# Holding activations instead of weights: a decoder layer on one core, with results kept with tokens on the partitions

## The chip, the core and the metric

The kernel runs on one core of a Trainium2 chip. Its five engines run their own instruction streams and wait for each other through semaphores: TensorE (matrix products, the profile's PE, with its loads of the stationary operand as PEld), VectorE (DVE), ScalarE (ACT), GpSimd (POOL) and SyncE (SP), which here issues nearly all loads. A matrix product holds one operand (stationary, up to 128 x 128) and moves the other past it (up to 512 columns), and writes to PSUM. The metric is device time in microseconds (us) of one execution.

## What is computed

One decoder layer for 256 tokens of 2048 features in f32. Cut to what matters:

```python
h = rmsnorm(x, ffn1_norm);  x = x + 0.5 * swiglu(h, ffn1_w_gate, ffn1_w_up, ffn1_w_down)   # 2048 -> 5632 -> 2048
h = rmsnorm(x, mix_norm);   proj = h @ w_in                                                # 2048 -> 9728
q_a, k_a, v_a, q_b, f_b, i_b, og_b, gate_a, gate_b = split(proj)
out_a = sliding_window_attention(rope(q_a), rope(k_a), v_a, sinks)                         # 256 x 1024
out_b = rmsnorm(hgrn2(q_b, f_b, i_b, lb)) * silu(og_b)                                     # 256 x 1024
merged = sigmoid(gate_a) * (out_a @ w_up_a) + sigmoid(gate_b) * (out_b @ w_up_b)
x = x + merged @ w_out
h = rmsnorm(x, ffn2_norm);  x = x + 0.5 * swiglu(h, ffn2_w_gate, ffn2_w_up, ffn2_w_down)
x = x + sigmoid(rmsnorm(x, ple_norm) @ ple_w_gate) * (p @ ple_w_proj)
return rmsnorm(x, final_norm)
```

## The kernel before

All weights stream through once, in a fixed order (`weight_order`), as 780 pieces of 128 x 1024 numbers (512 KB). `Weights.prep` loads a piece (SP), ScalarE rounds it to 12 bits (`whi`), VectorE takes the difference (`wlo`); `AHEAD = 4` pieces are prepared before the one in use, in rings of 6, 5 and 5 buffers. Activations are split the same way into two parts. A product is the sum of three: high by high, low by high, high by low.

There are two forms. In `chunk_b` and `pair_b` (through `mm_b`, L304, L306, L308) a 128 x 128 block of weights is stationary, and both parts of 256 tokens move past it as 512 columns, then past the low part of the weights as 256 columns. The result has features on the partitions and tokens along the row, which is the layout that the next product needs. `evac_b` adds the two halves and multiplies by the row factor of the norm, which `broadcast_cols` has laid out along the row (`rB`). In `block_a` (through `mm_a`, L270, L271, L276) a 128 x 128 block of activations is stationary and 512 weight columns move; the result has tokens on the partitions.

Gate, up and down of both feed-forwards, w_f, w_q, the two gates, w_up_a, w_up_b and w_out use the first form; w_i, w_og, w_kv, w_qa and the last stage the second. The residual x lies as `xT`, features on the partitions, until `natural` turns it with transposes (L778) before the last stage. `token_sums` adds squares over partitions with small matmuls (L231). The feed-forward runs in two slices of the 5632 columns: gate and up of a slice, then down of that slice, added to x. `next_stage` scales each finished part of x and splits it for the next product. While weights stream, `pump` advances attention and the recurrence, one step of each queue between two pieces, and `W.later(n, fn)` runs a step before the n-th piece from there.

Of the kernel before, what the change touches and what calls it, by code (L numbers as in the profile page):

```python
# [25 lines left out]
AHEAD = 4  # L26
PRIO = 3000
# [68 lines left out]
FF_SLICES = [(0, 24), (24, 44)]  # L96
MIX = (
    ("fq", 0), ("fq", 1), ("i", 0), ("og", 0), ("kv", 0), ("fq", 2),
    ("q", 0), ("fq", 3), ("q", 1), ("i", 1), ("og", 1),
)  # L100
GLOOK = 2


def weight_order():
# [9 lines left out]
    def ffn(n):  # L114
        if n == 1:
            for kg in range(4):
                for hf in range(2):
                    add("start", kg, hf)
        for a, b in FF_SLICES:
            for c in range(a, b):  # L120
                if n == 1 and c < 2:
                    continue
# [15 lines left out]
    for f in range(-GLOOK, KC):  # L138
        if f + GLOOK < KC:
            for w in ("w_ga", "w_gb"):  # L140
                for hh in range(2):
                    add(w, f + GLOOK, hh)
        if f >= 0:
            add("w_ua", f, 0)
            add("w_ub", f, 0)
    for fp in range(8):
        block("w_out", fp, 4)
# [8 lines left out]
def decoder_layer(ctx: ExitStack, tc: tile.TileContext, io, out):  # L156
# [17 lines left out]
    def atile(shape=(P, 2, S), dt=F32R, name="act"):  # L174
        return sb.tile(list(shape), dt, tag="act", name=uid(name), bufs=32)

    def etile(shape=(P, 2, S), name="e"):
        return sb.tile(list(shape), F32, tag="e", name=uid(name), bufs=4)
# [17 lines left out]
    xT = [sb.tile([P, 2, S], F32, tag=f"xT{i}", name=f"xT{i}") for i in range(8)]  # L196
    xc = lambda f: xT[f // 2][:, f % 2]
# [7 lines left out]
    def split_scaled(dst, src, g, vector=False):  # L205
        """dst[:, 0] + dst[:, 1] = src * g, each part of 12 bits."""
# [10 lines left out]
    def add_squares(ssq, src, first):  # L217
        """ssq += src ** 2, by feature."""
        if first:
            nc.scalar.activation(ssq, src, AF.Square)  # L220
        else:
            sq = gtile([P, 2, S], name="sq")
            nc.scalar.activation(sq, src, AF.Square)
            nc.vector.tensor_tensor(ssq, ssq, sq, op=ALU.add)

    def token_sums(ssq):
        """[128, 2, 1]: the sums over the features of each token, in PSUM."""
        ps = misc([P, 2, 2], uid("sq"))
        nc.vector.tensor_tensor(ssq[:, 0], ssq[:, 0], ssq[:, 1], op=ALU.add)
        for t in range(2):  # L230
            nc.tensor.matmul(ps[:, t], ssq[:, 0, t * P:(t + 1) * P], ones[:, 0:2], start=True, stop=True)  # L231
        return ps[:, :, 0:1]

    def inv_rms(ss, stage):
        """[128, 2]: 1 / sqrt(mean + eps) of each token."""
        r = const.tile([P, ss.shape[1]], F32, name=f"rstd{stage}")
        if ss.shape[2] > 1:
            nc.vector.tensor_reduce(r, ss, axis=AX.X, op=ALU.add)
        else:
            nc.vector.tensor_copy(r.unsqueeze(2), ss)  # L240
# [79 lines left out]
    def ffn(n, hT, rB_of, on_pair):  # L320
# [12 lines left out]
        for si, (a, b) in enumerate(FF_SLICES):  # L333
# [17 lines left out]
            for fp in range(8):  # L351
# [3 lines left out]
                if si == len(FF_SLICES) - 1:  # L355
                    on_pair(fp)
# [555 lines left out]
```

## Time and profile before

| | |
|---|---|
| time, median of 3 runs | 2264.26 us (2264.09 to 2264.36) |
| span of the profiled execution, first to last instruction | 2262.8 us |
| TensorE busy | 2245.5 us (99%), 12996 matmuls |
| loads of the stationary operand | 1943.7 us (86%), beside matmuls |
| VectorE, ScalarE, GpSimd busy | 1447.5 us (64%), 1090.3 us (48%), 11.8 us (1%) |
| moved from and to memory | 417.21 MB, 184 GB/s on average |
| granted TensorE clock | 0.999 of full speed |

The span begins with the first and ends with the last instruction that the profile shows; what lies around it is in the time and not in the span. Matmuls are pipelined: one starts before the one ahead has ended, so the distance between starts tells the cost, not the duration of one.

### The profile page before, as it was taken

What the parts mean: (1) busy time and instruction counts of PE and PEld (TensorE: products, weight loads), DVE (VectorE), ACT (ScalarE), POOL (GpSimd) and SP (SyncE); (2) the same over time, 40 slices, a digit from 0 to 9 for tenths busy, and PEclk for the clock granted to TensorE, in tenths of its full rate; (3) what the DMA queues carried; (4) which work ended last, traced back from release to release, by engine and by line L of the source; (5) the groups of instructions that cost most, each with busy time, mean ns of one, the idle gap of its engine ahead of it and who ended that gap; (6) DMA issues with size and microseconds to landing.
All of it is one profiled execution on the core that took longest, in us unless ns stands there. A gap on an engine that the chain in (4) does not pass through costs nothing.

```text
span 2262.8 us, 33350 instructions
## 1 busy us (share of the span) xinstructions
PE 2245.5 (99%) x12996; PEld 1943.7 (86%) x12996; DVE 1447.5 (64%) x2172; ACT 1090.3 (48%) x1590; POOL 11.8 (1%) x25
## 2 busy tenths in 40 slices
PE   8999999999999999999999999999999999999998
PEld 7888888888888878878888888888888888888887
DVE  7667655666666765776666677666665566666665
ACT  6455433444444445556445544544443344444444
POOL 0000000000000000000000000000000000000000
PEclk9999999999999999999999999999999999999999
DMA  7556565555665555444555555555555555556653
GB/s 276 191 189 192 186 190 188 187 188 187 188 190 190 177 159 168 159 133 157 186 186 187 187 189 188 187 188 187 188 189 191 186 186 186 188 189 215 186 179 110
DMA packets 116942, 417.21 MB, mean 184 GB/s; under 512 B 13616, under 2 KB 14000, under 8 KB 116784
## 3 DMA queue, kind: packets, MB, share of 16 engines
q1 hardware_dynamic: 115920, 413.74, 56.4%
q8 instruction: 102, 1.67, 0.3%
q10 hardware_dynamic: 864, 1.35, 0.2%
q14 instruction: 56, 0.46, 0.1%
HBM read 412.94 MB, written 2.10 MB: 183 GB/s over the span
## 4 chain that ended last, share of the span: by engine, by line
PE 99%; ACT 0%; issue 0%; DMA 0%; DVE 0%; SPq 0%; ACTq 0%; POOLq 0%; POOL 0%
PE pb L304 36%; PE pb L306 20%; PE pp L304 16%; PE pp L306 9%; PE pa L270 4%; PE pa L271 4%; PE pa L276 4%; PE pb L308 3%; PE pp L308 1%; PE lv L642 1%; PE st L304 1%; PE st L306 0%; PE sc L562 0%; DMA xT<-in_xT 0%; PE po L601 0%
## 5 line engine op out<-in xcount | busy, mean ns | idle before, releaser
L83 DVE TENSOR_TENSOR wlo<-raw,whi 128x1024 fp32r<-128x1024 f32 (+1 forms) x781 | 954.5, 1223 | 747.7 <-ACT whi L82 744.9
L82 ACT CAST whi<-raw 128x1024 fp32r<-128x1024 f32 (+1 forms) x781 | 818.4, 1049 | 1035.2 <-issue 252.6
L304 PE MATMUL pb<-hTf,whi 128*128 128x512 f32 x2580 | 710.6, 394 | 0.0
L304 PEld LDWEIGHTS pb<-hTf,whi 128*128 128x128 f32 x2580 | 449.6, 189 | 61.8
L306 PEld LDWEIGHTS pb<-hTf,wlo 128*128 128x128 f32 x2752 | 421.0, 188 | 59.0
L306 PE MATMUL pb<-hTf,wlo 128*128 128x256 f32 x2752 | 436.8, 280 | 0.0
L304 PE MATMUL pp<-act,whi 128*128 128x512 f32 x1344 | 369.2, 394 | 0.0
L304 PEld LDWEIGHTS pp<-act,whi 128*128 128x128 f32 x1344 | 233.0, 189 | 32.0
L306 PEld LDWEIGHTS pp<-act,wlo 128*128 128x128 f32 x1408 | 215.8, 189 | 30.2
L306 PE MATMUL pp<-act,wlo 128*128 128x256 f32 x1408 | 223.8, 281 | 0.0
L304 PE MATMUL pb<-hTmx,whi 128*128 128x512 f32 x720 | 200.2, 396 | 0.0
L304 PEld LDWEIGHTS pb<-hTmx,whi 128*128 128x128 f32 x720 | 124.8, 189 | 18.0 <-issue 0.7
L306 PEld LDWEIGHTS pb<-hTmx,wlo 128*128 128x128 f32 x768 | 117.4, 188 | 16.6
L306 PE MATMUL pb<-hTmx,wlo 128*128 128x256 f32 x768 | 121.8, 280 | 0.0
L270 PE MATMUL pa<-whi,hTmx 128*128 128x512 f32 x224 | 91.7, 409 | 0.0
L271 PE MATMUL pa<-whi,hTmx 128*128 128x512 f32 x224 | 87.7, 392 | 0.0
L314 DVE TENSOR_TENSOR ff<-ff,rBf 128x256 f32<-128x256 f32 x174 | 73.9, 425 | 5.7
L289 DVE SCALAR_TENSOR_TENSOR xT<-pp,xT 128x256 f32<-128x256 f32 x160 | 67.4, 422 | 7.7 <-PE pp L308 2.4
L312 DVE TENSOR_TENSOR ff<-pb,ff 128x256 f32<-128x256 f32 x172 | 71.9, 418 | 0.0
L308 PE MATMUL pb<-hTf,whi 128*128 128x512 f32 x172 | 68.1, 396 | 0.0
L304 PE MATMUL pp<-mT,whi 128*128 128x512 f32 x240 | 66.1, 394 | 0.0
L311 ACT COPY ff<-pb 128x256 f32<-128x256 f32 x172 | 63.1, 367 | 0.0
(234 smaller groups left out, 1683.2 us busy)
## 6 DMA issues: line engine op xcount, KB each, us to landing
raw<-in_ffn_down SPq DMA_DIRECT2D x176, 512.0 KB, 3.4
raw<-in_ffn_gate SPq DMA_DIRECT2D x172, 512.0 KB, 3.4
raw<-in_ffn_up SPq DMA_DIRECT2D x172, 512.0 KB, 3.3
raw<-in_w_ga SPq DMA_DIRECT2D x32, 512.0 KB, 3.4
raw<-in_w_gb SPq DMA_DIRECT2D x32, 512.0 KB, 3.3
raw<-in_w_out SPq DMA_DIRECT2D x32, 512.0 KB, 3.3
raw<-in_ple_gate SPq DMA_DIRECT2D x32, 512.0 KB, 4.3
raw<-in_w_f SPq DMA_DIRECT2D x16, 512.0 KB, 3.5
```

What stands on the lines that cost most here:

```text
L82: nc.scalar.copy(hi[:, c], raw[:, c])
L83: nc.vector.tensor_tensor(lo[:, c], raw[:, c], hi[:, c].bitcast(F32), op=ALU.subtract)
L270: nc.tensor.matmul(ps[t], ks[:, 0, tok], hi[:, c], start=(j == 0 and c == 0), stop=False)
L271: nc.tensor.matmul(ps[t], ks[:, 1, tok], hi[:, c], start=False, stop=False)
L276: nc.tensor.matmul(ps[t], ks[:, 0, tok], lo[:, c], start=False, stop=(last and c == 1))
L289: nc.vector.scalar_tensor_tensor(xc(f), ps[:, half * S:(half + 1) * S], scale, xc(f), op0=ALU.mult, op1=ALU.add)
L304: nc.tensor.matmul(ps, hi[:, c], mov(c), start=(first and c == 0), stop=False)
L306: nc.tensor.matmul(ps[:, 0:S], lo[:, c], mov(c)[:, 0], start=False, stop=False)
L308: nc.tensor.matmul(ps, hi[:, 3], mov(3), start=False, stop=True)
L311: nc.scalar.copy(dst, ps[:, S:2 * S])
L312: nc.vector.tensor_tensor(dst, ps[:, 0:S], dst, op=ALU.add)
L314: nc.vector.tensor_tensor(dst, dst, rB, op=ALU.mult)
```

## The change

The products of both feed-forwards, the gates, w_up_a, w_up_b and w_out go from the first form to `block_a`; w_f and w_q stay. x is kept with tokens on the partitions (`x[t][nb]`) and loaded a second time in that layout. `transpose_split` and `chunks` turn finished results with four transposes a burst, before they are split for the next product. The sums of squares come from ScalarE along the row, and the row factor is applied per partition. The first feed-forward starts with its first gate block in place of the pieces `start`, the tiles of xT for it rotate through three buffers, and the mixing stage begins with w_i. Tiles of activations are twice as large, 17 in place of 32.

```diff
-FF_SLICES = [(0, 24), (24, 44)]
+FF_SLICES = [(0, 6), (6, 11)]
-    ("fq", 0), ("fq", 1), ("i", 0), ("og", 0), ("kv", 0), ("fq", 2),
+    ("i", 0), ("fq", 0), ("fq", 1), ("og", 0), ("kv", 0), ("fq", 2),
-GLOOK = 2
+GATES = ((0, 1), (), (2,), (3,))
...
-                for w in ("gate", "up"):
-                    for h in range(2):
-                        add(f"ffn{n}_{w}", c, h)
-            for fp in range(8):
-                block(f"ffn{n}_down", fp, b // 4, a // 4)
+                block(f"ffn{n}_gate", c)
+                block(f"ffn{n}_up", c)
+            for nb in range(4):
+                block(f"ffn{n}_down", nb, 2 * b, 2 * a)
...
-    xT = [sb.tile([P, 2, S], F32, tag=f"xT{i}", name=f"xT{i}") for i in range(8)]
+    x = [[sb.tile([P, 512], F32, tag=f"x{t}{nb}", name=f"x{t}{nb}") for nb in range(4)] for t in range(2)]
...
+    def transpose_split(dst, srcs, kp):
+        pt = misc([P, 2, S], uid("tp"))
+        for c in range(2):
+            for t in range(2):
+                i = 2 * kp + c
+                nc.tensor.transpose(pt[:, c, t * P:(t + 1) * P], srcs[t][:, i * P:(i + 1) * P], ident)
+        nc.scalar.copy(dst[:, :, 0], pt)
+        nc.vector.tensor_tensor(dst[:, :, 1], pt, dst[:, :, 0].bitcast(F32), op=ALU.subtract)
...
+                pg = block_a(f"ffn{n}_gate", c, stat)
...
+                    for t in range(2):
+                        nc.scalar.activation(e[t], pg[t], AF.Silu, scale=r[:, t:t + 1])
+                pu = block_a(f"ffn{n}_up", c, stat)
...
+                for t in range(2):
+                    nc.vector.scalar_tensor_tensor(e[t], pu[t], r[:, t:t + 1], e[t], op0=ALU.mult, op1=ALU.mult)
+                for kp in range(2):
+                    acts[2 * c + kp] = at = atile()
+                    W.later(3 + kp, lambda at=at, e=e, kp=kp: transpose_split(at, e, kp))
+            for nb in range(4):
+                ps = block_a(f"ffn{n}_down", nb, lambda k: acts[2 * a + k // 2][:, k % 2], 2 * (b - a), 2 * a)
+                for t in range(2):
+                    nc.vector.scalar_tensor_tensor(x[t][nb], ps[t], 0.5, x[t][nb], op0=ALU.mult, op1=ALU.add)
+                if b == FF_SLICES[-1][1]:
+                    on_block(nb)
...
+        def chunks(nb, kp):
+            pt = misc([P, 2, S], uid("tx"))
+            for c in range(2):
+                for t in range(2):
+                    i = 2 * kp + c
+                    nc.tensor.transpose(pt[:, c, t * P:(t + 1) * P], x[t][nb][:, i * P:(i + 1) * P], ident)
+            for c in range(2):
+                f = 4 * nb + 2 * kp + c
+                split_scaled(hT[nb][:, 2 * kp + c], pt[:, c], gain[:, f:f + 1])
+        def on_block(nb):
+            for kp in range(2):
+                W.later(2 + kp, lambda kp=kp: chunks(nb, kp))
+            for t in range(2):
+                square_sum(ss[:, t, nb:nb + 1], x[t][nb])
+            if nb == 3:
+                r.append(inv_rms(ss, stage))
...
     def load_xt(i):
-        nc.sync.dma_start(xT[i], io["xT"][:, 2 * i:2 * i + 2, :])
+        xt = gtile(name="xt")
+        nc.sync.dma_start(xt, io["xT"][:, 2 * i:2 * i + 2, :])
...
+    for nb in range(4):
+        for t in range(2):
+            W.later(5 + 2 * nb + t, lambda t=t, nb=nb: load_x(t, nb))
...
+    for nb in range(4):
+        for g in GATES[nb]:
+            sga[g] = nat(block_a("w_ga", g, mov_h), AF.Sigmoid)
+            sgb[g] = nat(block_a("w_gb", g, mov_h), AF.Sigmoid)
+        if nb == 0:
+            W.drain()
...
+        pa = block_a("w_ua", nb, lambda k: out_a[k // 2][:, k % 2], 4)
...
+        for kp in range(2):
+            mT[2 * nb + kp] = m = atile(name="mT")
+            W.later(3 + kp, lambda m=m, e=e, kp=kp: transpose_split(m, e, kp))
+    for nb in range(4):
+        ps = block_a("w_out", nb, lambda k: mT[k // 2][:, k % 2])
+        for t in range(2):
+            nc.vector.tensor_tensor(x[t][nb], ps[t], x[t][nb], op=ALU.add)
+        on_block(nb)
...
-    for nb in range(4):
-        for t in range(2):
-            W.later(3 + 2 * nb + t, lambda t=t, nb=nb: natural(t, nb))
```

What one chunk of gate or up looks like on TensorE before, two pieces for 128 features (`pb` is its PSUM bank, `whi66` and `whi67` the high parts of the two pieces, `hTf1` the activations):

```order
L304 MATMUL pb_81_1955<-hTf10_81,whi66_1855 128x512 x4
L306 MATMUL pb_81_1955<-hTf10_81,wlo66_1856 128x256 x4
L304 MATMUL pb_81_1955<-hTf11_82,whi66_1855 128x512 x4
L306 MATMUL pb_81_1955<-hTf11_82,wlo66_1856 128x256 x4
L304 MATMUL pb_81_1955<-hTf12_83,whi67_1877 128x512 x4
L306 MATMUL pb_81_1955<-hTf12_83,wlo67_1878 128x256 x4
L304 MATMUL pb_81_1955<-hTf13_84,whi67_1877 128x512 x3
L306 MATMUL pb_81_1955<-hTf13_84,wlo67_1878 128x256 x4
L308 MATMUL pb_81_1955<-hTf13_84,whi67_1877 128x512
```

Sixteen matmuls a piece become twelve, all of 512 columns, in a block of eight pieces for 512 features. The end of such a piece on TensorE now, in an up block of the first feed-forward (`pa_35` and `pa_36` are the banks of the two token tiles), and the burst behind it (`ff_29`, `ff_30` hold the product of the block before):

```order
L241 MATMUL pa_36_823<-whi34_783,hTf11_82 128x512
L242 MATMUL pa_36_823<-whi34_783,hTf11_82 128x512
L247 MATMUL pa_35_822<-wlo34_784,hTf11_82 128x512
L247 MATMUL pa_36_823<-wlo34_784,hTf11_82 128x512
L247 MATMUL pa_35_822<-wlo34_784,hTf11_82 128x512
L247 MATMUL pa_36_823<-wlo34_784,hTf11_82 128x512
L284 MATMUL tp_38_891<-ident_64,ff_29_668 128x128
L284 MATMUL tp_38_891<-ident_64,ff_30_669 128x128
L284 MATMUL tp_38_891<-ident_64,ff_29_668 128x128
L284 MATMUL tp_38_891<-ident_64,ff_30_669 128x128
```

L241, L242 and L247 of the change are L270, L271 and L276 of before; the transposes are new there. On VectorE, at the end of the first down block of the second slice (its last piece is 233, `pa_135` and `pa_136` are its banks, `x00` and `x10` the two token tiles of x), the change has

```order
L84 TENSOR_TENSOR wlo237_4773<-raw237_4771,whi237_4772 128x1024
L317 SCALAR_TENSOR_TENSOR x00_73<-pa_135_4593,x00_73 128x512
L84 TENSOR_TENSOR wlo238_4799<-raw238_4797,whi238_4798 128x1024
L317 SCALAR_TENSOR_TENSOR x10_77<-pa_136_4594,x10_77 128x512
L84 TENSOR_TENSOR wlo239_4817<-raw239_4815,whi239_4816 128x1024
L202 SCALAR_TENSOR_TENSOR hTmx0_156<-tx_143_4821,vecs_65,hTmx0_156 128x256 x2
```

One split of weights stands between the two additions, and the parts of x for the next stage now come out of the transposes `tx`, which TensorE has behind piece 234.

## Rows read from the trace of the kernel before

**Rows 1.** The page: engines (part 1), chain that ended last (part 4).

```profile
PE 2245.5 (99%) x12996; PEld 1943.7 (86%) x12996; DVE 1447.5 (64%) x2172; ACT 1090.3 (48%) x1590; POOL 11.8 (1%) x25
...
PE 99%; ACT 0%; issue 0%; DMA 0%; DVE 0%; SPq 0%; ACTq 0%; POOLq 0%; POOL 0%
```

**Rows 2.** Waits of TensorE: engine and line, releaser, total us, times, longest.

```profile
PE st L304 <- ACT whi L82: 6.2, 1, 6.2
PE pt L587 <- DVE s L581: 1.5, 2, 0.7
```

**Rows 3.** TensorE in order of time, first feed-forward: start us, us, engine, instruction.

```profile
38.18 0.39 PE L308 MATMUL pb<-hTf,whi 128*128 128x512 f32 x1
...
106.57 0.63 PE L306 MATMUL pb<-hTf,wlo 128*128 128x256 f32 x4
107.04 1.09 PE L304 MATMUL pb<-hTf,whi 128*128 128x512 f32 x4
107.97 0.64 PE L306 MATMUL pb<-hTf,wlo 128*128 128x256 f32 x4
...
279.12 0.40 PE L308 MATMUL pb<-hTf,whi 128*128 128x512 f32 x1
```

**Rows 4.** The same view, down products of the first slice.

```profile
295.94 0.40 PE L308 MATMUL pp<-act,whi 128*128 128x512 f32 x1
...
413.72 0.40 PE L308 MATMUL pp<-act,whi 128*128 128x512 f32 x1
```

**Rows 5.** The same view, the last stage.

```profile
2183.20 1.07 PE L276 MATMUL pa<-wlo,hTpl 128*128 128x512 f32 x4
...
2191.36 0.84 PE L276 MATMUL pa<-wlo,hTpl 128*128 128x512 f32 x3
```

**Rows 6.** The same view, turning x; then its group (count, busy, mean ns).

```profile
2162.11 0.60 PE L778 MATMUL xn<-ident,xT 128*128 128x128 f32 x4
...
2178.09 0.60 PE L778 MATMUL xn<-ident,xT 128*128 128x128 f32 x4
...
L778 PE MATMUL xn<-ident,xT 128*128 128x128 f32 x32 | 4.8, 273 | 0.0
```

**Rows 7.** Groups by line, small matmuls of norms.

```profile
L231 PE MATMUL sq<-ones,ssq 128*128 128x2 f32 x16 | 2.0, 230 | 0.0
...
L251 PE MATMUL rb<-dg,ones 128*128 128x128 f32 x12 | 1.9, 278 | 0.0
```

**Rows 8.** Groups by line on VectorE.

```profile
L83 DVE TENSOR_TENSOR wlo<-raw,whi 128x1024 fp32r<-128x1024 f32 x779 | 953.2, 1224 | 747.4 <-ACT whi L82 744.6 <-DMA raw<-in_ffn_down 1.6 <-DMA pos<-in_pos 0.3
...
L211 DVE SCALAR_TENSOR_TENSOR hTf<-xT,vecs,hTf 128x256 fp32r<-128x256 f32 x32 | 14.7, 479 | 0.7 <-ACT hTf L210 0.5
...
L789 DVE TENSOR_TENSOR sgp<-pa,sgp 128x512 f32<-128x512 f32 x6 | 3.9, 683 | 0.2 <-ACT sgp L788 0.2
```

**Rows 9.** All engines in order of time, where a token-stationary block ends.

```profile
879.10 0.84 PE L304 MATMUL pb<-hTmx,whi 128*128 128x512 f32 x3
879.39 0.68 ACT L493 ACTIVATE nat<-pa,rstdmx 128x512 f32<-128x512 f32 x1
```

**Rows 10.** All engines in order of time, the start.

```profile
6.17 1.22 PE L304 MATMUL st<-hTf,whi 128*128 128x512 f32 x2 [6.17 <-ACT whi L82]
...
7.68 0.60 ACT L82 CAST whi<-raw 128x512 fp32r<-128x512 f32 x1
...
31.68 0.39 PE L308 MATMUL st<-hTf,whi 128*128 128x512 f32 x1
```

**Rows 11.** Stretches: busy us of engines, granted clock, DMA share, GB/s.

```profile
2155.30:2181.00 25.70, 25.70 (x132) 21.26 (x131) 15.41 (x20) 10.30 (x11) 0.70 (x1) 1.00 0.51 170
2183.20:2191.40 8.20, 8.20 (x38) 6.80 (x37) 5.68 (x6) 3.72 (x6) 0.00 (x0) 1.00 0.58 183
99.80:111.00 11.20, 11.20 (x66) 9.79 (x65) 7.09 (x10) 5.47 (x8) 0.00 (x0) 1.00 0.58 186
...
10.00:15.00 5.00, 5.00 (x25) 4.47 (x25) 5.00 (x10) 5.00 (x11) 0.00 (x0) 1.00 1.05 404
```

More of the change, by code (lines that the diff above doesn't have):

```diff
@@ L26 @@
 AHEAD = 4
+ACTS = 17
 PRIO = 3000
@@ L137, in weight_order @@
             block({"i": "w_i", "kv": "w_kv", "q": "w_qa", "og": "w_og"}[what], j)
[L138 to L147, printed above, removed]
+    for nb in range(4):
+        for g in GATES[nb]:
+            block("w_ga", g)
+            block("w_gb", g)
+        block("w_ua", nb, 4)
+        block("w_ub", nb, 4)
+    for nb in range(4):
+        block("w_out", nb)
     ffn(2)
@@ L521, in kv_block @@
         yield
-        kT.extend(atile([P, 2, S], F32, name="kT") for _ in range(2))
+        k2 = atile(dt=F32, name="kT")
+        kT.extend(k2[:, i] for i in range(2))
         for t in range(2):
@@ L552, in attend @@
         if t == 0:
-            for pr in range(2):
-                out_a[2 * g + pr] = atile(name="oa")
+            out_a[g] = atile(name="oa")
         s = etile([P, 4, P], name="s")
@@ L722, in decoder_layer @@
             W.queues[1].append(q_block(block_a("w_qa", j, mov_h), j))
-    def gate(name, f):
-        sg = sb.tile([P, S], F32, tag="sg", name=uid("sg"), bufs=6)
-        evac_b(sg, chunk_b(name, f, mov_h), rB)
-        nc.scalar.activation(sg, sg, AF.Sigmoid)
-        return sg
-    merged = []
-    sga, sgb = {}, {}
-    for f in range(-GLOOK, KC):
-        if f + GLOOK < KC:
-            sga[f + GLOOK] = gate("w_ga", f + GLOOK)
-            sgb[f + GLOOK] = gate("w_gb", f + GLOOK)
-        if f >= 0:
-            if f == 0:
-                W.drain()
-            e = etile(name="mg")
-            evac_b(e[:, 0], chunk_b("w_ua", f, lambda k: out_a[k], halves=1))
-            nc.vector.tensor_tensor(e[:, 0], e[:, 0], sga.pop(f), op=ALU.mult)
-            evac_b(e[:, 1], chunk_b("w_ub", f, lambda k: out_b[k], halves=1))
-            nc.vector.tensor_tensor(e[:, 1], e[:, 1], sgb.pop(f), op=ALU.mult)
-            nc.vector.tensor_tensor(e[:, 0], e[:, 0], e[:, 1], op=ALU.add)
-            m = atile(name="mT")
-            split(m, e[:, 0])
-            merged.append(m)
@@ L861, in _layout @@
     x = a["x"][0]
+    d["x"] = x.reshape(2, P, 4, 512).transpose(0, 2, 1, 3)
     d["xT"] = x.T.reshape(KC, P, S).transpose(1, 0, 2)
@@ L867, in _layout @@
     for n in (1, 2):
-        d[f"ffn{n}_gate"] = _pack_b(a[f"ffn{n}_w_gate"][0])
-        d[f"ffn{n}_up"] = _pack_b(a[f"ffn{n}_w_up"][0])
-        d[f"ffn{n}_down"] = _pack_p(a[f"ffn{n}_w_down"][0])
-    both = np.stack([a[n][0][:, 0:256].reshape(4, 4, P, 2, P) for n in ("ffn1_w_gate", "ffn1_w_up")])
-    d["start"] = both.transpose(1, 4, 3, 0, 2, 5).reshape(4, 2, P, 1024)
+        for part in ("gate", "up", "down"):
+            d[f"ffn{n}_{part}"] = _pack_a(a[f"ffn{n}_w_{part}"][0])
     w = a["w_in"][0]
@@ L879, in _layout @@
     d["w_og"] = _pack_a(w[:, 4608:5632])
-    d["w_ga"] = _pack_b(w[:, 5632:7680])
-    d["w_gb"] = _pack_b(w[:, 7680:9728])
-    d["w_ua"] = _pack_b(a["w_up_a"][0])
-    d["w_ub"] = _pack_b(a["w_up_b"][0])
-    d["w_out"] = _pack_p(a["w_out"][0])
+    d["w_ga"] = _pack_a(w[:, 5632:7680])
+    d["w_gb"] = _pack_a(w[:, 7680:9728])
+    d["w_ua"] = _pack_a(a["w_up_a"][0])
+    d["w_ub"] = _pack_a(a["w_up_b"][0])
+    d["w_out"] = _pack_a(a["w_out"][0])
     d["ple_gate"] = _pack_a(a["ple_w_gate"][0])
```

261 lines of the change are left out of this document (101 added, 160 removed).

## The prediction

> **What bounds the kernel now.** I read the chain that ended last first, with the busy shares [rows 1]: TensorE is 99% of the chain and busy 99% of the span, while VectorE stands at 64% and ScalarE at 48%. The waits of TensorE come next [rows 2]: 6.2 us for the first weights and 1.5 us inside attention, in a span of 2262.8 us. So nothing is waited for that could be removed; the time is the sum of TensorE's own instructions, and an edit counts by what it adds to that sum or takes from it. ScalarE and VectorE matter only where TensorE comes to wait for them.
>
> The third view is the order of time on TensorE. One "piece" is one 512 KB load of weights, 128 x 1024 numbers in two parts of 12 bits. With weights stationary (L304, L306, L308) a piece is 8 matmuls of 512 columns and 8 of 256. Between the ends of the first and the last whole gate or up chunk of the first feed-forward, 43 chunks of two pieces each lie from 38.18 to 279.12 us [rows 3]: 5.603 us a chunk, **2.802 us a piece**. Four 512-column matmuls start within 0.93 us and four 256-column ones within 0.47 us there, 0.2325 and 0.1175 us each. In the down products 7 chunk pairs of 6 pieces lie between 295.94 and 413.72 us, 2.804 a piece [rows 4].
>
> The kernel already has the other form: L270, L271 and L276 hold activations stationary and move 512 weight columns, 12 matmuls a piece. In the last stage three undisturbed pieces lie between 2183.20 and 2191.36 us [rows 5]: **2.720 us a piece**, 0.2267 a matmul. Both forms move 6144 columns a piece; the difference is 0.08 us.
>
> **The change part by part.**
>
> Conversions. Of the 780 pieces, 92 have the new form already and 32 (w_f, w_q) keep the old one. 656 change: 352 of gate and up, 64 of w_ga and w_gb, 176 of down, 32 of w_out, 32 of w_ua and w_ub. At 2.804 for down and 2.802 for the rest, 480 x 0.082 + 176 x 0.084 = 39.4 + 14.8 = **54.2 us off**. All of it is on the path, since TensorE never rests.
>
> Transposes added. A result with tokens on partitions must be turned before it can be a contraction again: 22 blocks of two bursts in the two feed-forwards (44), 4 blocks of two in the merge (8), 3 stages of 4 blocks of two in the residual (24). That is 76 bursts of 4 transposes of 128 x 128. Nothing in the trace is hidden behind a transpose on TensorE, so each burst counts in full. The price is at L778, where the kernel before puts one such burst after each piece of the new form: 5 pieces with 5 bursts lie between 2162.11 and 2178.09 us [rows 6], 3.196 us each, so a burst costs 3.196 - 2.720 = **0.476 us**. That is less than four times the 273 ns that the groups give for one transpose [rows 6], because they start before the one ahead has ended.
>
> Bursts removed. The 8 of L778 go, as x is kept with tokens on partitions all along. The sums of squares over partitions go (L231, 16 records in 4 bursts), and 2 of the 3 broadcasts of the row factor (L251, 12 records in 3 bursts) [rows 7]. I price these 14 like the others. Net 76 - 14 = 62 bursts, **29.5 us added**.
>
> Waits of the new transposes. A burst needs its block read out of PSUM. In the feed-forwards it stands two pieces (5.44 us) behind the end of its block, and VectorE has one multiply (683 ns for 128 x 512 out of PSUM), one split of weights (1224 ns) and the second multiply to do [rows 8]: 2.6 us, hidden. In the merge the chain is four such operations and two splits, where the second split also waits for the next piece: about 5.0 us, just hidden. In the three residual stages the burst stands only one piece (2.72 us) behind. There VectorE adds token tile 0 to x, splits one piece of weights, adds token tile 1. A reader of a finished block starts 0.29 us after the next piece's first matmul (879.39 against 879.10 [rows 9]); 0.29 + 0.683 + 1.224 + 0.683 = 2.88 us, and the transpose that needs it would start at 2.72 + 0.11 = 2.83 with its weights loaded some 0.2 before. So I expect 0.3 us of wait at each of 12 bursts, **3.6 us added**. Below, nothing (the split is moved behind); above, one more split in between: 12 x 1.5 = 18. I take the near end, since the order of VectorE shows one split there. What queues behind that wait is TensorE's next piece alone; the weights are four pieces ahead and don't run dry.
>
> The start. The first eight pieces run from 6.17 to 31.91 us (the last matmul starts at 31.68 and takes 0.23) [rows 10], 25.7 us where 8 x 2.80 = 22.4 are work: 3.3 us of stall. There piece 0 needed two tiles of xT; in the change it needs one, and the first square of x, which ScalarE took ahead of the second half of the weights (converted from 7.68 us on), moves behind piece 5. Piece 0 still waits for that half: its fifth matmul is due at 6.17 + 4 x 0.227 = 7.08, and 0.60 us after a start between 7.2 and 7.7 the half is ready at about 8.0, so 0.9 us are lost. I take **2.4 us off**, with bounds of 0 and 3.3. The tiles of xT now rotate through three buffers, so their loads queue on SP behind VectorE, and weights queue behind them; VectorE has 8 splits and 16 differences for the first 8 pieces, 8 x 1.22 + 16 x 0.48 = 17.5 us [rows 8], from about 5 us on, and TensorE needs the last of it near 27, so I take nothing for this.
>
> The second copy of x. Eight more loads of 256 KB go through SP's queue. At the 404 GB/s that the queues reached between 10 and 15 us [rows 11] they take 5.2 us of transfer, spread over pieces 5 to 28, where a piece needs 1.3 us of transfer in 2.72. Nothing to pay while weights are ahead; 5.2 us if that cover were gone.
>
> ScalarE and VectorE lose work: the additions to x in halves, the evacuations in 256-wide parts and the products by rB become fewer and wider. That is worth nothing, as neither is waited for. The first factor of the row norms now waits for squares of the late loads of x, and the transposes that need it stand inside piece 21, behind two multiplies and a split: 0 to 0.8 us by the durations above, I take 0.5. The two waits of attention (1.5 us [rows 2]) lie where the merge drained its queues; now 32 pieces of gates come first: 0.5 to 1 us off. These two cancel.
>
> Sum: -54.2 + 29.5 + 3.6 - 2.4 = -23.5 us. The page gives 2262.8 us for the span; the timed median is 2264.26, 1.5 us more, which lie outside the first and last instruction and stay. 2264.3 - 23.5 = **2240.8 us**, 1.0% faster; 0.2% (4.5 us) is about what a measurement of this kernel can tell from no change.
>
> **Rivals.**
>
> *The form isn't what is cheaper.* With weights stationary a matmul costs almost exactly by its columns, 0.2325 us for 512 and 0.1175 for 256 [rows 3]. If the 0.2267 of the other form [rows 5] belongs to the last stage and not to the form, a piece in the feed-forwards takes 12 x 0.2325 = 2.79 us, the conversions give 656 x 0.012 = 7.9 us, and the bursts win: 2264.3 - 7.9 + 29.5 + 1.2 = **2287 us**, slower. It decides at a gain of 0.047 us a piece, where gain and bursts are equal. For it: stages differ and the old form never ran in the last one. Against: the operands in the last stage have the shapes and the order of the change, and the granted clock was 1.00 there and in the feed-forward [rows 11]. The Trainium skill speaks for this rival (TensorE: Matmul & The Clock Gate, "Wait — 56ns, not 53.3ns?"): a warm matmul costs its columns at 2.4 GHz and about 2.5 ns more. By that a piece would take 2.599 us in the old form and 2.588 in the new, a gain of 7 us in all; the rows disagree with it, at 13 ns above the columns in the new form [rows 5] and 11 to 19 in the old [rows 3].
>
> *Transposes wait.* If the residual bursts meet a second split, or those of the feed-forwards wait too, the 3.6 us become 15 to 20: **2255 us**. For it: one piece of cover against a chain of 2.88 us. Against: the cover of all other bursts is twice as long.
>
> *A transpose costs its duration.* Four times 273 ns is 1.09 us a burst, 68 us for 62: 2264.3 - 54.2 + 68 + 1.2 = **2279 us**, slower. For it: the group's mean is a duration that the hardware reported. Against: the distance between pieces with a burst and without one, 0.476 us [rows 5, 6], and a granted clock of 1.00 (the level of 2.4 GHz) from 2155.3 to 2181 us, with 8 bursts in it [rows 11]. The Trainium skill (the same page, "Part 4: PE-mode transpose") gives about 275 ns for one transpose in the context of a kernel. The trace agrees with that as a duration [rows 6]; that starts lie closer is what decides between the two sums.
>
> *All goes well.* No waits at the bursts and a start without stall: -54.2 + 29.5 - 3.3 = -28, **2236 us** or a little less.
>
> That the change doesn't do what it says is excluded: the order of TensorE has 12 matmuls a piece and 304 transposes.
>
> **How the numbers follow.** The forecast case (2238 to 2248) 0.78, all well (2232 to 2238) 0.06, waiting transposes (2248 to 2262) 0.10, form not cheaper 0.05, durations 0.01. The range 2233 to 2251 takes the forecast, most of the good case and the first part of the waits. Faster 0.93, within 0.2% 0.01, slower 0.06.
>
> **What would show it.** The distance between pieces in the feed-forwards: 2.72 us right, 2.79 the first rival. A piece with a burst: 3.20 us. TensorE's waits: a row of tx bursts waiting for VectorE's addition to x, 12 times, some 0.3 us each. The end of piece 7 near 29 us. Busy shares of VectorE and ScalarE below 60% and 45%. The prediction is wrong above all if pieces without a burst take more than 2.74 us, or if tp bursts show waits at all.

## The result and the profile after

The changed kernel takes 2240.82 us (median of 4 runs, 2238.86 to 2242.16) against 2264.23 us (2264.09 to 2264.36) for the kernel before beside it: a ratio of 0.9895, 95% interval 0.9881 to 0.9909, 23.4 us less. The profiled execution is the fastest of the four, 2238.86 us with a span of 2236.9 us; against the 2262.8 us of the execution profiled before, its span is 25.9 us shorter.

The page of the changed kernel, engines (part 1) and the chain that ended last (part 4), beside [rows 1]:

```profile
PE 2220.7 (99%) x10620; PEld 1837.4 (82%) x10620; DVE 1204.4 (54%) x1416; ACT 1028.7 (46%) x1294; POOL 12.0 (1%) x25
...
PE 99%; ACT 0%; issue 0%; DMA 0%; DVE 0%; SPq 0%; ACTq 0%; POOLq 0%; POOL 0%
```

Its waits of TensorE (engine and line, releaser, total us, times, longest), beside [rows 2]:

```profile
PE pa L241 <- ACT whi L83: 5.5, 2, 5.3
PE pt L574 <- DVE s L568: 1.5, 2, 0.7
```

TensorE is still the whole chain. Its busy time fell by 24.8 us, and no burst of transposes, tp or tx, appears among its waits. The other engines lost work, VectorE from 64% to 54%, and nothing in the time answers to that.

Next, TensorE in order of time in the changed kernel, first feed-forward (start us, us, engine, instruction), beside [rows 3, 6]:

```profile
101.20 0.60 PE L284 MATMUL tp<-ident,ff 128*128 128x128 f32 x4
...
104.39 0.60 PE L284 MATMUL tp<-ident,ff 128*128 128x128 f32 x4
...
106.67 1.07 PE L247 MATMUL pa<-wlo,hTf 128*128 128x512 f32 x4
...
109.39 1.07 PE L247 MATMUL pa<-wlo,hTf 128*128 128x512 f32 x4
```

From burst to burst 3.19 us, from one piece's last four matmuls to the next's 2.72. So the piece has the price that the last stage showed before, and the burst costs 0.47. The same two numbers hold in every stage. Four stretches, from the start of the last matmul ahead of them to the start of their own last matmul, in us:

| stretch | before | after | change | by the prediction's terms |
|---|---|---|---|---|
| ffn1, first down products (48 pieces, 2 bursts) | 134.60 | 131.51 | -3.09 | -48 x 0.084 + 2 x 0.476 = -3.08 |
| ffn1, second gate and up (80 pieces, 8 bursts) | 224.14 | 221.39 | -2.76 | -80 x 0.082 + 8 x 0.476 = -2.75 |
| ffn1, second down products (40 pieces, 2 tp and 6 tx bursts) | 112.15 | 112.59 | +0.44 | -40 x 0.084 + 8 x 0.476 = +0.45 |
| gates and merge (96 pieces, 6 bursts) | 274.02 | 269.38 | -4.64 | -96 x 0.082 + 6 x 0.476 = -5.02 |

The last row is 0.4 off, where steps of attention run beside the products and may cross the stretch's ends. The third row shows the limit of the change: where every block of 10 pieces is followed by two bursts, the bursts cost more than the pieces give.

The start differs from what was forecast. TensorE in order of time in the changed kernel, the start (in brackets idle time before, and its releaser), beside [rows 10]:

```profile
5.27 0.80 PE L241 MATMUL pa<-whi,hTf 128*128 128x512 f32 x1 [5.27 <-ACT whi L83]
5.87 0.63 PE L242 MATMUL pa<-whi,hTf 128*128 128x512 f32 x1
6.29 0.63 PE L241 MATMUL pa<-whi,hTf 128*128 128x512 f32 x1
6.72 0.63 PE L242 MATMUL pa<-whi,hTf 128*128 128x512 f32 x1
7.55 0.79 PE L241 MATMUL pa<-whi,hTf 128*128 128x512 f32 x1 [0.21 <-ACT whi L83]
8.15 0.63 PE L242 MATMUL pa<-whi,hTf 128*128 128x512 f32 x1
...
9.43 1.10 PE L247 MATMUL pa<-wlo,hTf 128*128 128x512 f32 x4
```

The wait for the second half of the first weights is there, shorter than the 0.9 us forecast. But up to 9.43 us matmuls of 512 columns start 0.427 us apart, where later ones start 0.227 apart. The eighth piece ends at 29.42 us ("near 29" was forecast), 2.49 us earlier than before; 0.66 of that are the conversions of eight pieces, so the start itself gave 1.8 us here, not 2.4. Half of this is that the first product starts at 5.27 us in place of 6.17, which the prediction didn't have.

The kernel before has the wide spacing too (its TensorE in order of time):

```profile
9.79 1.05 PE L306 MATMUL st<-hTf,wlo 128*128 128x256 f32 x4
10.64 1.05 PE L304 MATMUL st<-hTf,whi 128*128 128x512 f32 x2
11.49 1.02 PE L306 MATMUL st<-hTf,wlo 128*128 128x256 f32 x4
12.35 1.53 PE L304 MATMUL st<-hTf,whi 128*128 128x512 f32 x6
```

Four matmuls of 256 columns take 0.85 us there, and two of 512 as much, until 12.35 us. Against the later spacing the first 16 matmuls lose 8 x 0.195 + 8 x 0.096 = 2.3 us, so most of the 3.3 us that the prediction read as a stall for data was this.

### The profile page after: what moved, and what is told of

It reads as the page before. It is cut to its first block, busy times and chain, and to the rows that moved or that the text cites. A ratio compares the mean times of both kernels' runs of the same rounds, so it can differ in the third digit from the quotient of the medians.

```text
span 2236.9 us, 27361 instructions
## 1 busy us (share of the span) xinstructions
PE 2220.7 (99%) x10620; PEld 1837.4 (82%) x10620; DVE 1204.4 (54%) x1416; ACT 1028.7 (46%) x1294; POOL 12.0 (1%) x25
## 4 chain that ended last, share of the span: by engine, by line
PE 99%; ACT 0%; issue 0%; DMA 0%; DVE 0%; SPq 0%; ACTq 0%; POOLq 0%; POOL 0%
PE pa L241 31%; PE pa L242 30%; PE pa L247 30%; PE pb L262 3%; PE pb L264 1%; PE tp L284 1%; PE lv L631 1%; PE tx L332 0%; PE sc L549 0%; DMA raw<-in_ffn_gate 0%; PE po L588 0%; PE pb L266 0%; PE pt L574 0%; ACT s L564 0%; ACT whi L83 0%
## 5 line engine op out<-in xcount | busy, mean ns | idle before, releaser
L241 PE MATMUL pa<-whi,hTf 128*128 128x512 f32 x1408 | 552.8, 393 | 5.5 <-ACT whi L83 5.5
L242 PE MATMUL pa<-whi,hTf 128*128 128x512 f32 x1408 | 549.0, 390 | 0.0
L247 PE MATMUL pa<-wlo,hTf 128*128 128x512 f32 x1408 | 376.8, 389 | 0.0
L241 PEld LDWEIGHTS pa<-whi,hTf 128*128 128x128 f32 x1408 | 264.9, 188 | 60.2 <-ACT whi L83 6.2
L247 PEld LDWEIGHTS pa<-wlo,hTf 128*128 128x128 f32 x1408 | 264.4, 188 | 55.1
L242 PEld LDWEIGHTS pa<-whi,hTf 128*128 128x128 f32 x1408 | 265.0, 188 | 53.9
L241 PE MATMUL pa<-whi,act 128*128 128x512 f32 x704 | 275.9, 392 | 0.0
L242 PE MATMUL pa<-whi,act 128*128 128x512 f32 x704 | 274.1, 389 | 0.0
L241 PE MATMUL pa<-whi,hTmx 128*128 128x512 f32 x480 | 192.1, 400 | 0.0
L247 PE MATMUL pa<-wlo,act 128*128 128x512 f32 x704 | 188.3, 389 | 0.0
L242 PE MATMUL pa<-whi,hTmx 128*128 128x512 f32 x480 | 187.4, 391 | 0.0
L247 PEld LDWEIGHTS pa<-wlo,act 128*128 128x128 f32 x704 | 132.2, 188 | 27.5
L242 PEld LDWEIGHTS pa<-whi,act 128*128 128x128 f32 x704 | 132.2, 188 | 26.9
L241 PEld LDWEIGHTS pa<-whi,act 128*128 128x128 f32 x704 | 132.2, 188 | 26.9
L247 PE MATMUL pa<-wlo,hTmx 128*128 128x512 f32 x480 | 128.4, 389 | 0.0
L241 PEld LDWEIGHTS pa<-whi,hTmx 128*128 128x128 f32 x480 | 90.1, 188 | 21.4 <-issue 2.5
L247 PEld LDWEIGHTS pa<-wlo,hTmx 128*128 128x128 f32 x480 | 90.1, 188 | 18.9
L242 PEld LDWEIGHTS pa<-whi,hTmx 128*128 128x128 f32 x480 | 90.2, 188 | 17.4
L262 PE MATMUL pb<-hTmx,whi 128*128 128x512 f32 x240 | 67.6, 400 | 0.0
L241 PE MATMUL pa<-whi,hTpl 128*128 128x512 f32 (+1 forms) x160 | 53.9, 348 | 0.0
```

The source lines that it names most:

```text
L241: nc.tensor.matmul(ps[t], ks[:, 0, tok], hi[:, c], start=(j == 0 and c == 0), stop=False)
L242: nc.tensor.matmul(ps[t], ks[:, 1, tok], hi[:, c], start=False, stop=False)
L247: nc.tensor.matmul(ps[t], ks[:, 0, tok], lo[:, c], start=False, stop=(last and c == 1))
L262: nc.tensor.matmul(ps, hi[:, c], mov(c), start=(first and c == 0), stop=False)
```

## Experiments

Differences in this section are to the kernel before as measured beside each run, whose medians were 2264.13 to 2264.48; the changed kernel stands at -23.4 above and at -23.6 in its second measurement.

### The changed kernel again, and without the second copy of x

No edit in `again`. In `no_x_copy`:

```diff
-        load_in_order(x[t][nb], io["x"][t, nb])
+        nc.gpsimd.memset(x[t][nb], 1.0)
```

> The changed kernel as it is, once more, for two things. (a) Its runs lay 3.3 us apart (2238.9 to 2242.2) where those of the kernel before lay 0.3 apart. Theory S1: the spread arises at the start, where the second copy of x is loaded beside the weights (DMA busy share near 1.0 from 20 to 40 us); then this profile, if its span is not 2236.9 again, has its difference before the first product of gate block 1, and the piece distances behind it are 2.72 as before. Theory S2: it arises all along (single matmuls or transposes that take a little longer in some runs); then the stage ends drift apart steadily. (b) The time: 2239 to 2242 us.

> The eight loads of the second copy of x are left out and the copy is filled with ones (so what is added to the residual, and the first norm factor, are not the reference's). Prediction's step: the copy costs nothing, so 2239 to 2242 us again. Theory S1 (the spread comes from these loads): runs within 0.5 us of one another and near 2238. Rival, that the loads delay weights at the start: 1 to 2 us less than the changed kernel, all of it before 45 us.

`again`: 2240.49 us (2239.62 to 2241.23), profiled span 2239.0. `no_x_copy`: 2240.08 us (2238.79 to 2241.13), -24.1. The copy costs nothing that can be measured, as forecast, and the spread stays without it. S1 named the right place and the wrong cause. The same stretch of the second profile of the unchanged text:

```profile
5.18 0.80 PE L241 MATMUL pa<-whi,hTf 128*128 128x512 f32 x1 [5.18 <-ACT whi L83]
...
8.21 0.79 PE L241 MATMUL pa<-whi,hTf 128*128 128x512 f32 x1 [0.95 <-ACT whi L83]
...
10.08 1.91 PE L247 MATMUL pa<-wlo,hTf 128*128 128x512 f32 x4
11.78 0.63 PE L241 MATMUL pa<-whi,hTf 128*128 128x512 f32 x1
...
12.96 0.39 PE L242 MATMUL pa<-whi,hTf 128*128 128x512 f32 x1
```

Here the fifth matmul starts 0.66 us later than in the first profile, since the half of the weights came later, and the wide spacing lasts until 12.64 us. Matched matmul by matmul, the second profile is 1.91 us behind at the 20th (13.88 against 11.97) and 2.1 us behind at the end. So nearly all that sets these two executions apart happens in the first 14 us, and S2, a drift along the way, is excluded for this pair.

### Gate and up in the old form

The block loop of gate and up, from the third block on, in both feed-forwards:

```diff
+                if c >= 2:
+                    for f in range(4 * c, 4 * c + 4):
+                        pg = chunk_b(f"ffn{n}_gateb", f, stat)
...
+                        split(acts[f // 2][:, f % 2], e[:, 1])
+                    continue
```

> Gate and up blocks 2 to 10 of both feed-forward stages go back to the form of before (288 pieces with the weights stationary, results with features on the partitions, no transposes: 36 bursts fewer); everything else is the changed kernel. By the terms of the prediction: 288 x 0.082 = +23.6 and 36 x 0.476 = -17.1, so +6.5 us: about 2247. Rival, that the form counts for nothing and the 26 us come from elsewhere: -17, about 2224. Rival, that bursts are hidden or nearly free and the form is all: +24, about 2264.

Measured 2248.54 us (2248.24 to 2249.26): +8.05 against `again`. The expectation forgot that the old form needs the row factor broadcast, once in each feed-forward: 2 more small bursts, about 1 us, makes 7.5; in its profile the first burst of the first feed-forward also waits 0.8 us for VectorE, which the changed kernel's doesn't. TensorE in order of time, from one chunk of two pieces to the next (the values come 5.61 us apart, 2.80 a piece):

```profile
200.61 1.09 PE L268 MATMUL pb<-hTf,whi 128*128 128x512 f32 x4
201.53 0.63 PE L270 MATMUL pb<-hTf,wlo 128*128 128x256 f32 x4
...
206.22 1.07 PE L268 MATMUL pb<-hTf,whi 128*128 128x512 f32 x4
```

Neither rival (-17, +24) is near. The form's gain and the bursts' price are both needed for +8, and the old price of a piece comes back with the old form, within a kernel that is otherwise the new one.

### No bursts in the feed-forwards

```diff
-                    W.later(3 + kp, lambda at=at, e=e, kp=kp: transpose_split(at, e, kp))
+                    W.later(3 + kp, lambda at=at, e=e, kp=kp: untransposed_split(at, e, kp))
```

> The 44 bursts of the two feed-forward stages are left out: the activations are split as they stand, with tokens on the partitions, and go untransposed into the down product (so the output is not the reference's); the splits by ScalarE and VectorE stay, now from SBUF. Prediction: 44 x 0.476 = 20.9 us less, about 2220. Rival, a transpose costs its duration (44 x 4 x 0.273 = 48 less): 2193. Rival, bursts lie beside other work: no change. If the bursts also cost waits for what they read, more than 20.9 comes back.

Measured 2219.54 us (2218.98 to 2219.95): 20.95 us less than `again`, where 20.9 was worked out. A burst costs 0.476 us, and neither its durations (48) nor hidden waits stand behind it.

### What makes the new form cheaper: the count of matmuls or the operand?

`lo_in_halves` and `moving_alternates` (in the latter the eight matmuls of the high parts are only reordered):

```diff
-                nc.tensor.matmul(ps[t], ks[:, 0, tok], lo[:, c], start=False, stop=(last and c == 1))
+                w = lo.shape[2]
+                for h in range(0, w, 256):
+                    nc.tensor.matmul(ps[t][:, h:h + 256], ks[:, 0, tok], lo[:, c, h:h + 256], start=False, stop=(last and c == 1 and h + 256 >= w))
```

```diff
-        for c in range(2):
-            ks = stat(2 * j + c)
-            for t in ts:
...
+        for t in ts:
+            tok = slice(t * P, (t + 1) * P)
+            for p in range(2):
+                for c in range(2):
...
```

> Same form as the changed kernel (tokens stationary, weight columns moving), but each matmul of the low weight parts is done as two of 256 columns: a piece is 8 matmuls of 512 and 8 of 256, the counts of the kernel before, with the operands of the kernel after. Some 748 pieces change. Theory T1 (the form before was dearer because 16 matmuls of mixed lengths carry more fixed time than 12 of one length): a piece takes 2.80, so 748 x 0.08 = +60 us, about 2300. Part of T1 alone (each matmul costs its columns and 13 ns, the mixing costs nothing): 2.72 + 4 x 0.013 = 2.77, +39, about 2280. Rival T2 (what counts is which operand is stationary): 2.72 stays, 2240.

> The 8 matmuls of the high parts in a piece are put in another order, so that no two neighbours stream the same weight columns (now each is streamed twice in a row). Counts, sizes and operands are those of the changed kernel. Rival T3 (the form after is cheaper because the moving operand is streamed twice in a row): a piece takes 2.79, +50 us, about 2290. T1: no change, 2240.

`lo_in_halves`: 2290.99 us (2290.24 to 2291.06), slower than before: ratio 1.0117, 1.0100 to 1.0134. That is 50.5 us above `again`, half way between T1's +60 and the +39 of its part. Its TensorE in order of time:

```profile
500.77 0.40 PE L241 MATMUL pa<-whi,hTf 128*128 128x512 f32 x1
...
502.61 1.11 PE L249 MATMUL pa<-wlo,hTf 128*128 128x256 f32 x8
503.56 0.40 PE L241 MATMUL pa<-whi,hTf 128*128 128x512 f32 x1
```

A piece takes 2.79 us with the operands of the new form and the lengths of the old. The eight of 512 columns take 1.84 (0.230 each, not 0.227), the eight of 256 take 0.95 (0.119 each), where four of 512 took 0.907. So of the 0.082 us that the change saves on a piece 0.07 are the count and the mix of lengths: 0.045 for four matmuls more, 0.028 for the long ones beside short ones. T1 stands, mixing included, though a little smaller than it was priced; T2 falls. About 0.01 a piece is left to what else differs between the forms (the old one also changes lengths four times in a piece, this run twice), and no run here separates it. The Trainium skill (TensorE: Matmul & The Clock Gate, "Wait — 56ns, not 53.3ns?") gives a fixed part of about 2.5 ns for a warm matmul; by that, as an estimate, four more would cost 0.010 us. The runs here disagree: they, with the stationary operand loaded anew for every matmul, show 0.045, and 0.073 with what the neighbours pay.

`moving_alternates`: 2242.57 us (2242.08 to 2243.42), -21.9. Its pieces take 2.72 as before, so T3 falls too. The median is 1.7 us above that of `again`, the span of the profiled execution 1.3. At the eighth piece's end only 0.2 of this is there: the third matmul already needs the second half of the first weights and starts 2.30 us after the second, but fewer matmuls behind it have the wide spacing. The other 1.1 us come at 69 us, where the first burst of the first feed-forward waits for VectorE. The first row shows this, the next two the same place in the changed kernel, on VectorE and on TensorE:

```profile
68.92 0.44 PE L282 MATMUL tp<-ident,ff 128*128 128x128 f32 x2 [0.97 <-DVE ff L308]
...
66.32 1.40 DVE L310 SCALAR_TENSOR_TENSOR ff<-pa,rstdf,ff 128x512 f32<-128x512 f32 x2
67.86 0.82 PE L284 MATMUL tp<-ident,ff 128*128 128x128 f32 x6
```

This is the burst that stands behind the first norm factor. In the changed kernel it doesn't wait, but it has only 0.14 us to spare: VectorE ends at 67.72 us, and the last six transposes start at 67.86.

### Where the forecast waits went

The prediction took 3.6 us for residual bursts that wait for VectorE's addition. They show no wait. All engines in order of time in the changed kernel, where a block of the residual ends, beside [rows 9]:

```profile
654.63 0.69 DVE L317 SCALAR_TENSOR_TENSOR x<-pa,x 128x512 f32<-128x512 f32 x1 [1.09 <-PE pa L247]
654.66 0.39 PE L241 MATMUL pa<-whi,act 128*128 128x512 f32 x1
...
655.24 1.22 DVE L84 TENSOR_TENSOR wlo<-raw,whi 128x1024 fp32r<-128x1024 f32 x1
...
656.37 0.69 DVE L317 SCALAR_TENSOR_TENSOR x<-pa,x 128x512 f32<-128x512 f32 x1
...
657.38 0.60 PE L332 MATMUL tx<-ident,x 128*128 128x128 f32 x4
```

The first addition starts 0.03 us before the next piece's first matmul, not 0.29 behind it: token tile 0 has its last product one matmul before the block's end. The three VectorE instructions start 0.61 and 1.13 us apart, closer than their durations. The second addition ends at 657.06, 0.32 us ahead of the burst. Two runs take that cover away. Both:

```diff
-                W.later(2 + kp, lambda kp=kp: chunks(nb, kp))
+                W.later(1 + kp, lambda kp=kp: chunks(nb, kp))
```

and the second also holds TensorE's order from the block's end through the next pieces (`pinned[0] = 3`, and each product and transpose there kept behind the one ahead of it in the program).

> The bursts of the residual stages are put one piece earlier: the first of a block stands right behind the block's last product, with no piece between. In the changed kernel these 24 bursts show no wait: VectorE's second addition to x ends 2.4 us after the next piece begins (657.05 against 654.66) and the burst is due at 657.38. Without that cover the whole chain is exposed at 12 bursts: 12 x (2.4 + about 0.1 to start) = +30 us, about 2270. If the additions then move ahead of the split of weights that now stands between them: 12 x 1.4 = +17, about 2257. Rival, the chain was never near the path: no change.

> Again the residual bursts one piece earlier, but now the order on TensorE is held: in the run before, the scheduler that writes the order had moved each early burst back among the products, to where its input was ready. Here four transposes stand directly behind the block's last product, twelve times, and the next piece stands behind them. By the trace of the changed kernel VectorE's second addition ends 2.4 us after the block's last product has begun its successor: 12 x (2.4 to 2.6) = +29 to +31 us against the changed kernel, about 2270. If VectorE overtakes nothing and the split that stands between the two additions isn't there yet: 12 x 1.4 = +17, about 2257. Rival, that a waiting burst is covered by what TensorE has queued: no change.

`tx_one_earlier`: 2241.75 us (2241.44 to 2242.98), -22.7 where -23.6 is unchanged. My +30 did not come, and the reason is not that the chain is short: in the order that TensorE got, the early transposes stand three to eleven products behind the block's end, each at a place where its half of x is ready (the first at 658.32 us, its input complete at 658.26). The scheduler that writes the order puts a burst behind products rather than let it wait. `tx_early_pinned`: 2276.62 us (2276.45 to 2276.84), +12.3, that is 36 above the changed kernel. Its waits of TensorE, then TensorE in order of time at one block's end, then a stretch (us; busy us of PE, PEld, DVE, ACT, POOL; granted clock; DMA share; GB/s):

```profile
PE tx L339 <- DVE x L324: 15.7, 16, 1.4
PE tx L339 <- DVE x L739: 7.9, 8, 1.4
```

```profile
748.15 1.07 PE L254 MATMUL pa<-wlo,act 128*128 128x512 f32 x4
749.78 0.33 PE L339 MATMUL tx<-ident,x 128*128 128x128 f32 x1 [0.56 <-DVE x L324]
751.51 0.90 PE L339 MATMUL tx<-ident,x 128*128 128x128 f32 x3 [1.40 <-DVE x L324]
...
753.07 0.63 PE L248 MATMUL pa<-whi,hTmx 128*128 128x512 f32 x1
753.49 0.63 PE L249 MATMUL pa<-whi,hTmx 128*128 128x512 f32 x1
```

```profile
752.00:754.00 2.00, 2.00 (x7) 1.61 (x7) 1.37 (x5) 1.16 (x4) 1.25 (x3) 0.50 0.70 244
```

At each of the 12 blocks the first transpose starts 0.95 us behind the product ahead of it and the second 1.73 behind the first, where 0.23 and 0.11 are usual: 12 x 2.34 = 28.0 us, close to the 29 to 31 of the first theory. The rest is a cost that I had not counted: at four of the twelve blocks the granted clock is at its lower level after the wait (0.50 of full speed, 1.2 of 2.4 GHz), and 4 to 7 matmuls start 0.427 us apart. These 25 cost 25 x 0.2 = 5.0 us. About 3 us stay unassigned, part of it the start, which is never the same. So the chain behind a block is real, though shorter than the prediction had it (2.4 us from the next piece's first matmul in the changed kernel, not 2.88), and here one piece of cover is worth 3 us a block.

### The start, and joined bursts

`warm_start` (also in `warm_in_order` and `both_edits`), `warm_in_order` besides, and `bursts_of_8` (also in `both_edits`; the bursts of the residual and the merge alike):

```diff
+    wp = misc([P, S], "wp")
+    for _ in range(9):
+        nc.tensor.matmul(wp[:, 0:P], ones, ones, start=True, stop=True)
```

```diff
-        nc.sync.dma_start(xt, io["xT"][:, 2 * i:2 * i + 2, :])
+        d = nc.sync.dma_start(xt, io["xT"][:, 2 * i:2 * i + 2, :])
+        if i == 1:
+            tc.keep_in_program_order(d)
```

```diff
-                    W.later(3 + kp, lambda at=at, e=e, kp=kp: transpose_split(at, e, kp))
+                    W.later(3, lambda at=at, e=e, kp=kp: transpose_split(at, e, kp))
```

> Nine matmuls of ones by ones (fp32, 128 x 128, into a bank that nobody reads) stand on TensorE ahead of the first product, where it waits 5.2 us for the first weights. Theory S3: the spread of the runs and 2 to 3 us are lost at the start, where the first 10 to 15 matmuls of 512 columns start 0.427 us apart, not 0.227, for a time that differs from run to run (until 9.4 us in one profile, 12.6 in the next); with TensorE busy from 1 us on, that time runs out earlier: 2 to 3 us less, 2237 to 2239, and the runs closer together. Rival, the slow starts come from the data's arrival or from the transfers beside them: no change, 2240.5.

> Two edits at the start: the nine matmuls on ones as in warm_start, and the second tile of xT is kept behind the second half of the first weights in the queue of loads (it went ahead of it; piece 0 doesn't need it). In the profiles so far TensorE waits 0.2 to 2.1 us inside piece 0 for that half, and that wait is what is left of the spread once the slow first matmuls are gone. Theory S4: the half lands earlier, the wait goes: 1 us less than warm_start, about 2238.5, and the runs within 1 us. Rival, the landing of all early loads varies and the wait moves to piece 1: 2239.5 and the same spread.

> The two bursts of a block are put together, 8 transposes in a row, 38 times. Starts inside a burst lie 0.109 us apart; the rest of the 0.476 us (0.04) is the change of kind and back. If that is paid once for each interruption: 38 x 0.04 = -1.5 us, about 2239. Rival, that the second half of a burst waits for a bank or for the reading of the first: more, up to 38 x 0.5 = +19.

> The two edits that helped, together: the bursts of a block joined (8 transposes in a row), and nine matmuls on ones ahead of the first weights. By the rows of the two runs: joined bursts 38 x 0.03 = -1.1 us, matmuls at the slow spacing at the start -1 to -2 us where the first weights are there in time. Against the changed kernel's 2240.5 that makes 2237 to 2238.5. Rival, the edit of the start is worth nothing in the median since the wait for the first weights varies by as much: 2238.5 to 2239.5, as with joined bursts alone.

| kernel | median us (range of 4 runs) | to before |
|---|---|---|
| warm_start | 2239.72 (2239.03 to 2241.72) | -24.8 |
| warm_in_order | 2239.90 (2239.64 to 2242.42) | -24.4 |
| bursts_of_8 | 2238.51 (2237.02 to 2239.49) | -25.8 |
| both_edits | 2237.58 (2237.39 to 2237.82) | -26.8, ratio 0.9881 (0.9865 to 0.9898) |

The start of `both_edits`, TensorE in order of time:

```profile
1.02 4.21 PE L184 MATMUL wp<-ones 128*128 128x128 f32 x18 [1.02 <-POOL ones L181]
5.18 0.80 PE L244 MATMUL pa<-whi,hTf 128*128 128x512 f32 x1
5.78 0.63 PE L245 MATMUL pa<-whi,hTf 128*128 128x512 f32 x1
...
8.10 0.50 PE L244 MATMUL pa<-whi,hTf 128*128 128x512 f32 x1 [0.99 <-ACT whi L83]
8.43 0.39 PE L245 MATMUL pa<-whi,hTf 128*128 128x512 f32 x1
```

With TensorE busy from 1.02 us on (the nine matmuls show as 18 records), the wide spacing ends inside piece 0: with the first matmul in the profile of `warm_start`, after the fourth here. The wait for the second half of the weights stays. So S3 is right that work ahead of the first weights shortens the wide spacing. What that is worth in the end isn't settled: the median is 0.8 us below that of `again`, where 2 to 3 were forecast, and the runs of either kernel lie further apart than that. The profile of `warm_start` shows where a part goes. Its eighth piece ends at 28.75 us, 0.7 us ahead of the first profile of the changed kernel and 2.6 ahead of the second. Then the first burst of the first feed-forward waits, as in `moving_alternates`:

```profile
68.45 0.44 PE L287 MATMUL tp<-ident,ff 128*128 128x128 f32 x2 [0.55 <-DVE ff L313]
```

Of the lead over the first profile 0.55 us are gone at 71 us and 0.75 at 285. The same burst waits 1.00 us in `warm_in_order` and 1.31 in `both_edits`. S4 finds no support: with the order of the loads held, the wait moved on (0.26 us in piece 0 and 0.20 in piece 1), and the median is no better. What is left of the spread in `warm_start` and `warm_in_order` (2.7 and 2.8 us) isn't explained, as only one execution of each is profiled; that `both_edits` shows 0.4 us in four runs is too little to call it cured.

Joined bursts: at 101 us two single bursts add 3.081 + 3.193 + 2.833 - 3 x 2.720 = 0.947 us to their three pieces, and one of eight adds 3.520 + 2.847 - 2 x 2.720 = 0.927 to its two. That is 0.02 us less, and it stays so up to 714 us; from 742 us on, a joined pair saves 0.05 to 0.07. Matched matmul by matmul with the first profile of the changed kernel, all of them together save 1.7 us behind the start, where 1.5 was forecast. The median moved by 2.2, of which the start, different again, can hold the rest. No row shows a wait for the second half. `both_edits` is faster than either kernel of this study by its median, 3.2 us less than the changed kernel.

## Why the prediction held

Forecast 2240.8 us, measured 2240.82 and 2240.49. By its own steps:

- **Conversions, -54.2.** Right: pieces of 2.72 us in every stage, and the stretches of the table above to 0.02 us where only pieces and bursts change. The rival of the form fell, but what it leans on was half true: it isn't which operand is stationary that counts, or for no more than 0.01 of the 0.08 us. The lengths and the count of matmuls do, which the prediction never said. It took the price from a stage that happened to have the same lengths.
- **Transposes, +29.5.** Right: 20.95 us for 44 bursts, 0.476 each. The rival of durations is out by more than a factor of two.
- **Waits of the residual bursts, +3.6.** Mis-sized: 0. The step that failed is "a reader of a finished block starts 0.29 us after the next piece's first matmul". In [rows 9] ScalarE came to its read from another instruction, so 0.29 was its own delay, not the bank's (ScalarE in order of time, kernel before):

```profile
878.43 1.05 ACT L82 CAST whi<-raw 128x1024 fp32r<-128x1024 f32 x1
```

That makes 0.32 us of difference; another 0.17 is that VectorE's three instructions start closer than their durations, which the prediction added up. The mechanism is real, as the pinned run shows, but here it leaves a margin of 0.32 us.
- **The start, -2.4.** Mis-sized: -1.8 in the first profile and +0.1 in the second (whose eighth piece ends 1.9 us later). The step that failed is the reading of 3.3 us in [rows 10] as stall for data: about 2.3 of them are matmuls at the wide spacing, which the change doesn't remove, and which lasts until 9.43 us in one execution and 12.64 in another. What the start did give is in part the first product's earlier start.
- **Attention and the first norm factor, -0.5 to -1 and +0.5.** Both 0 in the changed kernel: the 1.5 us wait of attention is unchanged, and the stretch from the eighth piece to the end of the first gate and up (88 pieces, 10 bursts added, 2 removed) changed by -3.25 us where -88 x 0.082 + 8 x 0.476 = -3.4. But the margin of 0.14 us behind the norm factor is thin: in seven of the edited kernels this burst waits, 0.2 to 1.3 us, so the prediction named a real place.
- **The second copy of x, 0.** Right, by `no_x_copy`.

By measured terms the first profile should be -54.2 + 29.5 - 1.8 = -26.5 us and the second -54.2 + 29.5 + 0.1 = -24.6; their spans are 25.9 and 23.8 us shorter, so 0.6 to 0.8 us stay unassigned. The forecast was right by its two large terms. That it hit the median to 0.1 us is luck: 3.6 us of waits that did not come stand against 2.4 us of start that came in part in one execution and not at all in another.

## What to carry to other kernels

Where one engine is 99% of the chain, cost a change by the distance between starts in undisturbed rows of the same lengths, and ask which of these lengths change: 12 matmuls of 512 columns beat 8 and 8 of 512 and 256 by 0.07 us a piece here, with the same operand held. A result in the wrong layout costs 0.47 us per burst of four transposes, which pays off if 6 or 7 pieces of that saving stand against each burst. A reader on another engine should be timed from the matmul that finishes its own bank, not from the end of the block; and one piece of other work between a block and its transposes was worth 3 us a block here. A gain at the start can be lost again at the next place without margin, so it should be read at the end of the program and not where it is made.

## What the runs showed of the hardware beyond that

At the start, matmuls of 512 columns are 0.427 us apart, which is 512 columns at 1.2 GHz. The Trainium skill (TensorE: Matmul & The Clock Gate, "Wait — 56ns, not 53.3ns?") gives 426.7 ns for a cold array; the trace agrees, at 426 to 427 ns. But the granted clock in the profile reads 1.00 there (a stretch of the changed kernel: us; busy us of PE, PEld, DVE, ACT, POOL; granted clock; DMA share; GB/s):

```profile
6.00:8.00 2.00, 1.79 (x5) 0.98 (x4) 1.46 (x4) 0.62 (x1) 0.00 (x0) 1.00 0.92 332
```

In the pinned run the same spacing comes with 0.50. So the column misses the slow start, and the distance between starts is the safer reading. In the pinned run eight of twelve waits of the same length left the clock up and four did not; what decides between them isn't settled here.

After a burst, the next matmuls of 512 columns stay up to 9 ns slower than usual for some six matmuls (0.231, 0.236, 0.228, 0.233, 0.231, until 0.227 returns). That tail is part of the 0.476 us; the long matmuls behind short ones in `lo_in_halves` start at such distances too (0.230 on average).
